# Block sums formed a slice per group, a second output tile begun early, and three smaller moves in a transformer trunk

## The chip, the cores and the metric

The kernel runs on one core of one Trainium2 chip. A core has TensorE (PE, with its weight loads as PEld), VectorE (DVE), ScalarE (ACT), GpSimd (POOL) and SyncE (SP, which here issues most of the transfers). The metric is the device time of one execution in microseconds; less is better.

## The reference

One pre-norm layer with D = 1024 and 2048 tokens, all in float32:

```python
xn = rms_norm(x, mix_norm_g[l]);  h = xn @ w_in[l]
q, k, v, f_logit, z = jnp.split(h, ...)             # 8 heads of 64; z has 2 x 512
log_f = jax.nn.log_sigmoid(f_logit + b_f[l])
attn = forgetting_attention(q, k, v, log_f)         # logit + cumsum(log f)[t] - cumsum(log f)[s], causal
sgu = spatial_gating(jax.nn.gelu(z), ...)           # zu * (chunk-causal mix of layer_norm(zv) + b)
merged = concat([rms_norm(attn, g_a), rms_norm(sgu, g_b)])
x = x + merged @ w_out[l]
gate, up = jnp.split(rms_norm(x, ffn_norm_g[l]) @ w_gate_up[l], 2)
x = x + (silu(gate) * up) @ w_down[l]               # d_ff = 2816
return rms_norm(x, final_norm_g)
```

## The kernel before

**Arithmetic.** Each float32 operand is split into a high and a low part (`hi_of`, a cast, mostly on ACT, L129; `lo_of`, the remainder, on DVE, L132), and each product is three matmuls: high by high, high by low, low by high. The program writes operations in an order of its own; a scheduler places them on each engine's queue, held by `behind(...)`, which names an instruction that has to come first, and by the buffers of the tile pools. An engine runs its queue in order.

**Projections (0 to about 350 us).** Four chunks of 512 tokens. In each, eight tiles of q and k (`L576`), the v tiles (`L458`) and the forget gates are formed. From chunk 1 on, the maxima of the attention logits of the chunk before are taken between the k steps of these tiles: `one_max` is one matmul (L361) and one reduction on DVE (L363 or L366); its operands A, B and D are read back from DRAM where q, k and the gate rows were stored shortly before. `n_early` is the number of maxima per tile, worked out from the table `EB`.

**Attention (to about 960 us).** `units` lists pairs of a head h and a query chunk j; each has 4j + 4 steps, one per block of 128 keys, 320 in all. A step is the logits (L735, L736, bank `mx_ps`), the exponential on ACT (`Pt`, L738), its split (`Ph` on ACT, `Pl` on DVE), on the diagonal blocks an affine select of each on POOL (L748), and two steps later the product with V (L768 to L773, tile `tp`). As filler between the steps TensorE gets the gating projection (`gates`, L927), whose side work `u_side` transposes the gated tiles `zr` into bank `z`, copies them on ACT into `wsth` or `wstl` (one buffer each, L998) and stores them to ST. From step `OPEN` the preparation of the first two output tiles (`out_prep`) runs, one `yield` per step: normalised rows are squared on ACT (L1092), POOL adds the squares (L1094, L1095), TensorE sums them over partitions (L1108) and broadcasts the root (L1113). Tile 0's product with the left half of `w_out` is begun between the last steps (`out_product`, `pz`). The other output tiles follow (`out_tiles`), and `out_done` turns each into normalised columns, stored to XT (to about 1098 us).

**FFN (from about 1098 us).** Up and Down run as products of 2 x 2 blocks with seven products and block sums in place of eight. There are five sets: 1 and 2 are Up for one half of the tokens each (22 items, in groups of two), 3, 4 and 5 are Down for a third of d_ff each (8 items). In a group each of the seven slots has two items of 12 matmuls (9 in set 5). The moving operands R0 to R6 (high and low) stay for a whole set and are refilled in its last group for the next: `staged` loads the four blocks of 1 MB into `sg0` to `sg3`, and `refill` splits blocks and forms their sums there on DVE and POOL (L1352, table `TE`). The weights of a group (`raw`, or HD in Down) are loaded some groups ahead, their sums formed (L1352) and split. `evac` takes a finished product from its bank `pp`; `done` (queued in `posts`) forms the last RMSNorm of a tile of rows: square on ACT (L1515), root on DVE and POOL, scaling on DVE (L1540), store.

## Time and profile before

| | |
|---|---|
| median of three executions | 2375.95 us (2375.18 to 2379.35) |
| the profiled execution | 2381.17 us |
| its span, first to last instruction | 2379.4 us |
| granted TensorE clock, mean | 0.996 |
| busy share: PE, DVE, ACT, POOL | 98%, 70%, 44%, 26% |
| HBM traffic | 253 MB read, 125 MB written |

In a row of the timeline stand the start, the duration (for xN from the first start to the last end), the engine, the line, the operation, what it writes <- what it reads, and in brackets the idle time of the engine before it and what ended that. "issue" as the one who ended a wait means that the profile shows none. SPq is SP's queue of transfers.

### The profile page before, as it was taken

The numbers are of one execution on the slowest core, as the hardware profiler recorded it, in microseconds if no ns is written. First come the engines' busy times: TensorE is split into PE (matmuls) and PEld (weight loads), VectorE is DVE, ScalarE is ACT, GpSimd is POOL, SyncE is SP. The second block draws the span as 40 slices with busy tenths as digits, with TensorE's granted clock in tenths as the row PEclk, the third lists the DMA queues.
The fourth block names the chain that finished last, engine by engine and source line by source line (L and its number), as shares of the span: only waits on it lengthen the run. The fifth ranks groups of instructions, "written<-read, shape, count | busy, mean of one in ns | idle before, by whom it ended". The sixth has DMA issues, their size and how long they took to land. (4 is left out here: it accounts for less than half of the span.)

```text
span 2379.4 us, 31425 instructions
## 1 busy us (share of the span) xinstructions
PE 2340.1 (98%) x10582; PEld 1894.4 (80%) x10582; DVE 1669.8 (70%) x2736; ACT 1055.7 (44%) x1770; POOL 623.3 (26%) x705
## 2 busy tenths in 40 slices
PE   9999999999999989999999999999999999999997
PEld 7778777777777768788888888788888878888886
DVE  6658668888888666467655656965555696696888
ACT  5322138777787766344323233432323242332433
POOL 1100012122121222221323323232322325354531
PEclk9999999999999999999999999999999999999999
DMA  8845667655687865666233232423232245455453
GB/s 271 284 154 193 205 206 207 180 161 156 191 211 237 223 206 168 216 214 199 71 89 92 80 94 76 151 83 89 72 89 82 80 141 186 167 186 200 152 190 148
DMA packets 358152, 380.60 MB, mean 160 GB/s; under 512 B 22292, under 2 KB 275924, under 8 KB 355432
## 3 DMA queue, kind: packets, MB, share of 16 engines
q1 hardware_dynamic: 342008, 335.36, 46.6%
q0 software_dynamic: 7616, 27.33, 3.3%
q10 hardware_dynamic: 8368, 15.91, 1.8%
q8 instruction: 85, 1.39, 0.3%
q14 instruction: 75, 0.61, 0.1%
HBM read 253.35 MB, written 125.18 MB: 159 GB/s over the span
## 5 line engine op out<-in xcount | busy, mean ns | idle before, releaser
L129 ACT CAST wh<-raw 128x512 fp32r<-128x512 f32 (+2 forms) x492 | 302.1, 621 | 748.3 <-PE pp L1663 608.3
L132 DVE TENSOR_TENSOR wl<-raw,wh 128x512 fp32r<-128x512 f32 (+2 forms) x496 | 373.2, 762 | 82.0 <-ACT wh L129 81.5
L1663 PE MATMUL pp<-wl,wh 128*128 128x512 f32 x1056 | 325.4, 389 | 1.2 <-ACT u L1418 1.0
L1663 PE MATMUL pp<-wh,wh 128*128 128x512 f32 x1056 | 325.4, 389 | 0.0
L1352 POOL TENSOR_TENSOR raw<-raw 128x512 f32<-128x512 f32 (+1 forms) x124 | 163.6, 1321 | 510.0 <-DMA raw<-in_w_gu_dram 357.9
L132 DVE TENSOR_TENSOR Pl<-Pt,Ph 128x512 fp32r<-128x512 f32 (+1 forms) x320 | 195.2, 615 | 80.4 <-ACT Ph L129 77.5
L1663 PEld LDWEIGHTS pp<-wl,wh 128*128 128x128 f32 x1056 | 198.1, 188 | 43.0 <-ACT u L1418 1.4
L1663 PEld LDWEIGHTS pp<-wh,wh 128*128 128x128 f32 x1056 | 198.2, 188 | 41.2
L738 ACT ACTIVATE Pt<-mx_ps 128x512 f32<-128x512 f32 (+1 forms) x320 | 169.2, 533 | 124.9 <-PE mx_ps L736 120.7
L1663 PE MATMUL pp<-wl,wl 128*128 128x512 f32 x528 | 205.8, 390 | 1.0 <-DVE wl L132 1.0
L1663 PE MATMUL pp<-wh,wl 128*128 128x512 f32 x528 | 205.4, 389 | 0.0
L927 PE MATMUL z<-wh,xz 128*128 128x512 f32 x496 | 188.9, 397 | 0.0
L1352 DVE TENSOR_TENSOR raw<-raw,raw 128x512 f32<-128x512 f32 (+1 forms) x112 | 132.1, 1181 | 77.7 <-POOL raw L1352 74.2
L129 ACT CAST Ph<-Pt 128x512 fp32r<-128x512 f32 (+1 forms) x320 | 175.9, 557 | 19.3 <-PE tp L770 3.8
L363 DVE TENSOR_REDUCE mx<-mx_ps 128x1 f32<-128x512 f32 x192 | 129.9, 682 | 20.5 <-PE mx_ps L361 20.0
L748 POOL TENSOR_SCALAR_AFFINE_SELECT Ph<-Ph 128x128 fp32r<-128x128 f32 x128 | 52.8, 413 | 314.4 <-DVE Pl L132 219.6
L768 PE MATMUL tp<-Ph,V 128*128 128x512 f32 (+1 forms) x320 | 118.8, 371 | 3.7 <-POOL Ph L748 2.6
L735 PE MATMUL mx_ps<-A,D 74*128 74x512 f32 (+1 forms) x320 | 119.3, 373 | 2.9 <-ACT Pt L738 2.9
L361 PE MATMUL mx_ps<-D,A 66*128 66x512 f32 (+2 forms) x320 | 118.6, 373 | 2.6 <-issue 2.0
L773 PE MATMUL tp<-Pl,V 128*128 128x512 f32 (+1 forms) x320 | 118.6, 370 | 1.3 <-POOL Pl L748 0.9
L736 PE MATMUL mx_ps<-B,C 128*128 128x512 f32 (+1 forms) x320 | 117.5, 368 | 0.0
L1663 PEld LDWEIGHTS pp<-wl,wl 128*128 128x128 f32 x528 | 99.1, 188 | 22.6 <-DVE wl L132 2.1
(340 smaller groups left out, 5301.7 us busy)
## 6 DMA issues: line engine op xcount, KB each, us to landing
raw<-in_w_gu_dram SPq DMA_DIRECT2D x88, 512.0 KB
xz<-XS SPq DMA_DIRECT2D x31, 1024.0 KB
HD<-hT SPq DMA_DIRECT2D x44, 512.0 KB
D<-KH SPq DMA_DIRECT2D x112, 128.0 KB
XA<-xa SPq DMA_DIRECT2D x27, 512.0 KB
raw<-HD SPq DMA_DIRECT2D x24, 512.0 KB
XA<-xb SPq DMA_DIRECT2D x21, 512.0 KB
xa<-XA SPq DMA_DIRECT2D x20, 512.0 KB
```

What stands on the lines that cost most here:

```text
L129: return nc.scalar.copy(o, i) if eng is nc.scalar else eng.tensor_copy(o, i)
L132: return eng.tensor_tensor(o, i, f(h), ALU.subtract)
L361: last_mx.append(nc.tensor.matmul(pm[:, 0:n], lhs, Dt[0 : lhs.shape[0], 0:n], start=True, stop=True))
L363: nc.vector.tensor_reduce(mx[:, a, s : s + 1], pm, AX.X, ALU.max)
L735: nc.tensor.matmul(st[:, off:], Dt[:, b * P : (b + 1) * P], A[:, off:], start=True, stop=False)
L736: nc.tensor.matmul(st[:, off:], C[:, b * P : (b + 1) * P], B[:, off:], start=False, stop=True)
L738: nc.scalar.activation(Pt[:, off:], st[:, off:], AF.Exp)
L768: nc.tensor.matmul(pv[:, off:], V[:, 0:P], Ph[:, off:], start=kb == 0, stop=False)
L773: nc.tensor.matmul(pv[:, off:], V[:, 0:P], Pl[:, off:], start=False, stop=kb == 4 * j + 3)
L927: nc.tensor.matmul(pz, xz[a][:, k, :], w[b][:, k, :], start=n == 0, stop=n == 3 * KT - 1)
L1352: (nc.vector if e == "v" else nc.gpsimd).tensor_tensor(o, a, b, op)
L1663: nc.tensor.matmul(pm, a[:, k, :], b[:, k, :], start=on is None and k == 0 and e == 0, stop=k == it.kh - 1 and e == 2, skip_group_check=n ...
```

## The change

**Maxima.** In chunk 1 the first q tile (pr = 0) takes no maxima; the others take four per tile instead of three.

**Order of units and opening.** The last eight units were heads 6, 7 as 7's j = 0, 1, then 6's four, then 7's j = 2, 3. Now they are (6,0), (7,0), (6,1), (7,1), (6,2), (6,3), (7,2), (7,3). The output preparation opens at step 260, not 265, and has more pauses where it has its own buffer.

**Second output tile.** The left half of tile 1 is also begun between the last steps: its eight products, an own load of its x (`x01[1]`), and its addition.

**Last gating tiles.** For the last q of `u_side` the four transposed tiles go through `mx_ps` banks and into four parts of one tile (tag `zvh`) instead of `wsth` and `wstl`.

**Block sums.** The sums of a set's blocks are no longer formed in its refill. In the groups of sets 1 and 2, `block_sums` takes one slice k of all four blocks in each of 15 rounds: four loads into two `xa` tiles, four operations on DVE, and in the next group two stores to the DRAM tile `SM`. The refill fetches seven ready blocks (three of w_down or XT, four of SM: the fourth of these for the position that formerly came last of the sums), four ahead and three in place of blocks already kept.

**Tail.** In the last group the posts run in another number per slot, held behind the last evacuation of each slot.

The matmuls are the same in number and kind.

```diff
-EB = [1, 12, 12, 12]
+EB = [1, 11, 12, 12]
-OPEN = 265
+OPEN = 260
...
-                    with behind(*maxima(n_early, k)):
+                    with behind(*maxima(n_early if c > 1 or which or pr else 0, k)):
...
+        last = q == NCH - 1
+        if last:
+            z4 = T(p2z, [P, 4, 4, P], F32, "zvh", bufs=1)
         for cc in range(4):
...
-            tp = T(psz, [P, 4, P], F32, "z", bufs=NZ)
+            tp = T(ps2, [P, 4, P], F32, "mx_ps", bufs=NMX) if last else T(psz, [P, 4, P], F32, "z", bufs=NZ)
...
-            sT = T(p2z, [P, 4, P], F32, ("wsth", "wstl")[cc % 2], bufs=1)
+            sT = z4[:, cc] if last else T(p2z, [P, 4, P], F32, ("wsth", "wstl")[cc % 2], bufs=1)
...
-    units = units[:-8] + units[-4:-2] + units[-8:-4] + units[-2:]
+    units = units[:-8] + [(h, j) for j in range(2) for h in (H - 2, H - 1)] + units[-6:-4] + units[-2:]
...
         for _ in range(2 if wg and left else 0):
-            out_product(pz, 0, 0, left.pop(0), s0)
-            if not left:
-                nc.vector.tensor_tensor(x0, x0, pz, ALU.add)
+            t, k = left.pop(0)
+            if k == K_OUT[0]:
+                pz = T(psz, [P, CH], F32, "z", bufs=NZ)
+                if t:
+                    x01.append(T(p2, [P, CH], F32, "jk", bufs=1))
+                    ld(x01[1], x[P : 2 * P, 0:CH])
+            out_product(pz, t, 0, k, None if t else s0)
+            if k == K_OUT[-1]:
+                nc.vector.tensor_tensor(x01[t], x01[t], pz, ALU.add)
...
+    def source(s, n):
+        if n in (0, 2, 6):
+            return block(s, {0: 0, 2: 2, 6: 3}[n])
+        return SM[s][:, {1: 0, 4: 1, 5: 2, 3: 3}[n], 0 : sets[s - 1][0].kh]
...
+    def block_sums():
+        last = None
+        for s in (2, 3, 4, 5):
+            for k in range(sets[s - 1][0].kh):
+                n, p = yield
+                while n != 2 or NF // 2 < p < NF // 2 + 2:
+                    n, p = yield
+                if last:
+                    with behind(hd[-1]):
+                        put(*last)
+                while n != 3 or NF // 2 - 1 <= p < NF // 2 + 2:
+                    n, p = yield
+                t = [T(xap, [P, D], F32, "xa") for _ in range(2)]
+                b = [t[i // 2][:, (i % 2) * CH : (i % 2 + 1) * CH] for i in range(4)]
+                with behind(*hd[-1:]):
+                    for i in range(4):
+                        ld(b[i], block(s, i)[:, k])
+                while n != 5:
+                    n, p = yield
+                tt("v", b[1], b[3], b[1], ALU.subtract)
+                tt("v", b[0], b[0], b[1], ALU.add)
+                n, p = yield
+                tt("v", b[2], b[2], b[0], ALU.subtract)
+                tt("v", b[3], b[3], b[0], ALU.subtract)
+                last = s, k, t
...
-    def refill(sg, kh, te):
-        ...
-        yield keep(0, b11)
-        tt(te[1], b11, b11, b12, ALU.add)
-        yield keep(1, b11)
-        yield keep(2, b21)
-        tt(te[2], b21, b21, b11, ALU.subtract)
-        tt(te[3], b11, b22, b11, ALU.subtract)
-        yield keep(3, b11)
-        ...
+    def refill(s, sg):
+        kh = sets[s - 1][0].kh
+        for n in range(7):
+            r = keep_as(n, sg[n], kh)
+            if n < 3:
+                sg.append(fetch(s, n + 4))
+            yield r
...
-        for _ in range(len(its)):
-            while posts and next(posts[0], 0) == 0:
-                posts.pop(0)
+        tail = p == len(grp) - 1
+        with behind(*[its[0].last] if tail and n else ()):
+            for _ in range((2, 2, 2, 2, 0, 1, 1)[n] if tail else len(its)):
+                while posts and next(posts[0], 0) == 0:
+                    posts.pop(0)
+            if tail and n == 6:
+                next(posts.pop(), None)
```

Three places show what moves. The first is DVE in the last group of set 2, where the operands of set 3 are formed: `sg` are the blocks, `R1l`, `R3l`, `R4l` (and the tiles named `wh`, `wl` of 128x2048) the low halves kept, `u` and `c` products in work. Before:

```order
L132 TENSOR_TENSOR wh_12188<-sg_3821_15724,wh_12188 128x2048
L1465 TENSOR_TENSOR u_18288<-u_18288,pp_18309 128x512
L1465 TENSOR_TENSOR u_18292<-u_18292,pp_18322 128x512
L1352 TENSOR_TENSOR sg_3821_15724<-sg_3821_15724,sg_3822_15725 128x2048
L132 TENSOR_TENSOR wl_18343<-raw_4243_18163,wh_18342 128x512
...
L132 TENSOR_TENSOR R1l_18339<-sg_3821_15724,R1h_18338 128x2048
...
L1352 TENSOR_TENSOR sg_3823_15726<-sg_3823_15726,sg_3821_15724 128x2048
L132 TENSOR_TENSOR wl_18421<-raw_4243_18163,wh_18420 128x512
L1352 TENSOR_TENSOR sg_3821_15724<-sg_3824_15727,sg_3821_15724 128x2048
```

Now:

```order
L131 TENSOR_TENSOR wh_12192<-sg_4142_17576,wh_12192 128x2048
L1519 TENSOR_TENSOR u_18473<-u_18473,pp_18496 128x512
L1519 TENSOR_TENSOR u_18477<-u_18477,pp_18509 128x512
L131 TENSOR_TENSOR wl_18531<-raw_4278_18348,wh_18530 128x512
L131 TENSOR_TENSOR wl_18535<-raw_4280_18352,wh_18534 128x512
L131 TENSOR_TENSOR R1l_18525<-sg_4143_17578,R1h_18524 128x2048
```

The three sums of 128x2048 are gone; the weights' splits (`wl` from `raw`) and those of R1 follow the evacuations at once.

The second is POOL at the opening of the output tiles: `zvl` are the squares of tiles 0 and 1, `rar` their roots, `Ph` and `Pl` the selects of the last diagonal steps. Before:

```order
L1094 TENSOR_TENSOR zvl_9643<-zvl_9643 128x256
L1095 TENSOR_TENSOR zvl_9643<-zvl_9643 128x128
L748 AFFINE_SELECT Ph_9778<-Ph_9778 128x128
L748 AFFINE_SELECT Pl_9780<-Pl_9780 128x128
L748 AFFINE_SELECT Ph_9792<-Ph_9792 128x128
L748 AFFINE_SELECT Pl_9794<-Pl_9794 128x128
L177 TENSOR_TENSOR rar_9807<-raa_9805,mhalf_206 128x1
L748 AFFINE_SELECT Ph_9820<-Ph_9820 128x128
L748 AFFINE_SELECT Pl_9822<-Pl_9822 128x128
L1094 TENSOR_TENSOR zvl_9643<-zvl_9643 128x256
L1095 TENSOR_TENSOR zvl_9643<-zvl_9643 128x128
```

Now:

```order
L1097 TENSOR_TENSOR zvl_9526<-zvl_9526 128x256
L1098 TENSOR_TENSOR zvl_9526<-zvl_9526 128x128
L1097 TENSOR_TENSOR zvl_9526<-zvl_9526 128x256
L1098 TENSOR_TENSOR zvl_9526<-zvl_9526 128x128
L748 AFFINE_SELECT Ph_9778<-Ph_9778 128x128
L748 AFFINE_SELECT Pl_9780<-Pl_9780 128x128
L176 TENSOR_TENSOR rar_9791<-raa_9789,mhalf_206 128x1
L176 TENSOR_TENSOR rar_9797<-raa_9795,mhalf_206 128x1
```

Both pairs of additions stand ahead of the last four diagonal steps; before, tile 1's pair stood behind three of them.

The third is DVE at the end of the program: `sg2` is the last tile of rows, `r4a` the start of a root, L1540 (now L1596) the scaling of a finished row tile. Before:

```order
L1540 SCALAR_TENSOR_TENSOR xa_4836_21443<-xa_4836_21443,r4r_4933_21851,sg0_4715_20896 128x1024
L1420 TENSOR_TENSOR u_4931_21847<-u_4931_21847,pp_4936_21859 128x512
L175 TENSOR_SCALAR r4a_4939_21884<-ss4_4937_21871 128x1
L1352 TENSOR_TENSOR sg2_4930_21844<-sg2_4930_21844,u_4931_21847 128x512
L1540 SCALAR_TENSOR_TENSOR sg1_4894_21697<-sg1_4894_21697,r4r_4940_21886,sg0_4715_20896 128x1024
L1423 TENSOR_TENSOR sg2_4930_21844<-sg2_4930_21844,pp_4929_21834 128x512
L1425 TENSOR_TENSOR sg2_4930_21844<-sg2_4930_21844,pp_4941_21890 128x512
L1510 TENSOR_SCALAR a5_4942_21901<-a5_4942_21901 128x1
L1511 TENSOR_TENSOR sg2_4930_21844<-sg2_4930_21844,sg0_4715_20896 128x512
L175 TENSOR_SCALAR r4a_4947_21921<-ss4_4944_21906 128x1
L1540 SCALAR_TENSOR_TENSOR sg1_4894_21697<-sg1_4894_21697,r4r_4948_21923,sg0_4715_20896 128x1024
L1427 TENSOR_TENSOR u_4931_21847<-u_4931_21847,pp_4946_21909 128x512
```

Now:

```order
L1596 SCALAR_TENSOR_TENSOR xa_4880_21635<-xa_4880_21635,r4r_4977_22043,sg0_4759_21088 128x1024
L1474 TENSOR_TENSOR u_4975_22039<-u_4975_22039,pp_4982_22054 128x512
L1415 TENSOR_TENSOR sg2_4974_22036<-sg2_4974_22036,u_4975_22039 128x512
L174 TENSOR_SCALAR r4a_4983_22066<-ss4_4978_22047 128x1
L1477 TENSOR_TENSOR sg2_4974_22036<-sg2_4974_22036,pp_4973_22026 128x512
L1596 SCALAR_TENSOR_TENSOR sg1_4938_21889<-sg1_4938_21889,r4r_4984_22068,sg0_4759_21088 128x1024
L174 TENSOR_SCALAR r4a_4987_22085<-ss4_4985_22072 128x1
L1564 TENSOR_SCALAR a5_4990_22102<-a5_4990_22102 128x1
L1565 TENSOR_TENSOR sg2_4974_22036<-sg2_4974_22036,sg0_4759_21088 128x512
L1596 SCALAR_TENSOR_TENSOR sg1_4938_21889<-sg1_4938_21889,r4r_4988_22087,sg0_4759_21088 128x1024
L1479 TENSOR_TENSOR sg2_4974_22036<-sg2_4974_22036,pp_4989_22091 128x512
L1481 TENSOR_TENSOR u_4975_22039<-u_4975_22039,pp_4992_22107 128x512
```

Between the start of a root and the scaling that needs it stands now an addition or the square's own work, and the last scaling comes one addition earlier (ahead of L1479, before behind L1425).

## The prediction

> **What bounds the kernel now.** I read the page's first part, the stages in the view of windows, TensorE's waits for the whole span, then the windows and timeline around its longest gaps. A windows row gives: stretch, its length, busy us and count of PE, PEld, DVE, ACT and POOL, granted clock, DMA share, GB/s.

> ```profile
> PE 2340.1 (98%) x10582; PEld 1894.4 (80%) x10582; DVE 1669.8 (70%) x2736; ACT 1055.7 (44%) x1770; POOL 623.3 (26%) x705
> 0.00:350.00 350.00, 345.05 (x1550) 274.11 (x1551) 238.13 (x589) 117.35 (x172) 37.95 (x78) 1.00 0.66 219
> 350.00:962.00 612.00, 600.50 (x2848) 470.69 (x2847) 478.32 (x924) 450.80 (x821) 133.84 (x298) 0.99 0.69 193
> 1098.00:2379.40 1281.40, 1261.26 (x5549) 1040.72 (x5547) 873.93 (x1116) 434.76 (x697) 426.05 (x294) 1.00 0.39 124
> ```

> TensorE is busy 2340.1 of 2379.4 us, and the change takes no matmul away. What can be won is its 39.3 us of idle time (5.0 in the projections, 11.5 in the attention, 20.1 from the FFN to the end) and stretches at a lower clock. The idle time sits in few places; a row of waits gives total, times, longest:

> ```profile
> PE pp L1663 <- DVE wl L132: 4.0, 4, 2.3
> PE mx_ps L735 <- ACT Pt L738: 2.9, 4, 2.1
> PE pp L1663 <- ACT wh L129: 2.7, 2, 1.4
> PE mx_ps L1108 <- POOL zvl L1095: 2.2, 2, 1.3
> PE mx_ps L361 <- issue: 2.0, 1, 2.0
> PE pp L1663 <- ACT u L1418: 1.0, 1, 1.0
> ```

> A gap of two microseconds costs more than itself. Over the last stage a matmul takes 1261.26 / 5549 = 0.227 us. After the 2.02 us gap before the first maximum, two starts lie 0.43 us apart:

> ```profile
> 86.95 0.30 PE L361 MATMUL mx_ps<-D,A 66*128 66x128 f32 x1 [2.02 <-issue]
> ...
> 88.58 0.63 PE L576 MATMUL mm<-xh,wh 128*128 128x512 f32 x1
> 89.01 0.63 PE L576 MATMUL mm<-xl,wh 128*128 128x512 f32 x1
> ```

> The granted clock (third figure from the end) shows the same at three other places, and none of it behind a gap of 1.3 us at 1524:

> ```profile
> 840.00:850.00 10.00, 8.54 (x36) 6.57 (x36) 6.46 (x12) 5.77 (x11) 2.63 (x6) 0.83 0.16 45
> 870.00:880.00 10.00, 7.98 (x28) 6.38 (x29) 2.12 (x5) 3.94 (x8) 1.28 (x4) 0.83 0.74 237
> 1520.00:1525.00 5.00, 3.68 (x16) 2.47 (x14) 5.00 (x5) 1.33 (x3) 3.03 (x1) 1.00 0.68 209
> 1955.00:1960.00 5.00, 4.96 (x15) 3.95 (x16) 5.00 (x6) 1.84 (x3) 1.11 (x1) 0.66 0.65 218
> ```

> 0.17 of 10 us, or 0.34 of 5 us, is 1.7 us lost each time; with four places 6.8 us.

> [...]

> **First maximum a tile later.** TensorE stands at 86.95 because the maximum's operands are still arriving. With none in the first tile of chunk 1, it comes 21 matmuls later, 21 x 0.227 = 4.8 us, past the 2.0. Removed: 2.0 + 1.7 = −3.7. The rest of the chunk takes four maxima per tile instead of three, whose loads have one unit's lead; bounds −3.7 to +1 (one more 2.0 wait without a dip, say half of it net). I take −3.7, as the lead left (2.8 us) is longer than the gap.

> **Second tile early, unit order, opening five steps sooner.** Two places. In the output preparation TensorE waits for POOL's sums:

> ```profile
> 835.30 0.94 POOL L1094 TENSOR_TENSOR zvl<-zvl 128x256 f32<-128x256 f32 x1 [14.57 <-ACT zvl L1092]
> 837.10 0.38 PE L1108 MATMUL mx_ps<-ones_c,zvl 128*128 128x1 f32 x2 [1.29 <-POOL zvl L1095]
> 840.98 0.38 PE L1108 MATMUL mx_ps<-ones_c,zvl 128*128 128x1 f32 x2 [0.89 <-POOL zvl L1095]
> 842.64 0.40 PE L1113 MATMUL mx_ps<-ident,rar 128*128 128x128 f32 x1 [0.57 <-POOL rar L177]
> ```

> 1.29 + 0.89 + 0.57 = 2.75, plus the 1.7 behind 840. The changed order puts both pairs of sums ahead of the last diagonal selects and gives one more pause before each reader; a pause is about one attention step (612 us for 320 of them, 1.9), more than the longest wait. I keep 0.5 of the waits: −3.9 (bounds −4.4 and 0). Second:

> ```profile
> 860.00:866.00 6.00, 4.88 (x22) 2.60 (x22) 5.45 (x12) 5.23 (x13) 1.02 (x1) 1.00 0.91 271
> 870.88 0.58 ACT L998 COPY wsth<-z 128x512 f32<-128x512 f32 x1 [3.05 <-DMA ST<-wsth]
> 872.02 0.44 PE L735 MATMUL mx_ps<-A,D 74*128 74x384 f32 x1 [2.10 <-ACT Pt L738]
> ```

> ScalarE's copy of a gating tile waits 3.05 us for the store that reads its buffer; the exponential queued behind it is late and TensorE waits 2.10. With a buffer for each of the last four copies this wait cannot arise. The attention steps there also get 24 products more as filler (24 x 0.227 = 5.4 us of matmuls that stood in one run later, so no time of their own). 2.1 + 1.7, and half of the 1.1 us that TensorE idles in 860 to 866, is −4.3 (bounds −4.9 and 0). The added load of 256 KB, one add of 0.7 us on DVE and a copy on ScalarE lie beside these products. Against it: the twelve diagonal steps, whose selects on POOL come between exponential and product, now stand in one row instead of two; TensorE waits for these selects 2.6 + 0.9 us in the whole run, of which I let a fifth come again: +0.7.

> **Block sums.** At the end of a set DVE forms the next set's operands from whole blocks (ns: least, median, most):

> ```profile
> L1352 DVE TENSOR_TENSOR sg<-sg,sg x19: 1218/2279/3418, 1019.5 to 2239.2; 128x2048 f32<-128x2048 f32 x14, 128x1536 f32<-128x1536 f32 x3, 128x1024 f32<-128x1024 f32 x2
> 1912.00:1960.00 48.00, 43.97 (x185) 35.29 (x184) 47.34 (x42) 22.19 (x26) 14.83 (x8) 0.96 0.47 154
> 1950.94 4.04 DVE L132 TENSOR_TENSOR wl<-raw,wh 128x512 fp32r<-128x512 f32 x3
> 1955.04 0.50 PE L1663 MATMUL pp<-R3h,wl 128*128 128x512 f32 x1 [2.31 <-DVE wl L132]
> ```

> DVE is the late engine at the end of set 2: busy 47.34 of 48 us, while TensorE idles 4.0 and waits for DVE's splits. Three sums go, at 2.28 at least 6.8 us of DVE, against the 2.31 that its longest wait is late. All waits of pp together are 4.0 + 2.7 + 1.0 = 7.7, plus the dip's 1.7: 9.4 if every one goes. I take −8.3, one wait of about 1 us staying (bounds −9.4 and 0).

> The work returns in 15 rounds: four loads of 256 KB, four sums of 128x512 and two stores of 512 KB each; in all 60 sums, 103 more DMA issues on SP. The nearest rows for a round are these of an Up group:

> ```profile
> 1214.19 4.74 SPq L1481 DMA_DIRECT2D HD<-hT  x2
> 1223.86 0.69 DVE L1465 TENSOR_TENSOR u<-u,pp 128x512 f32<-128x512 f32 x1 [1.43 <-PE pp L1663]
> 1226.36 0.62 ACT L129 CAST wh<-raw 128x512 fp32r<-128x512 f32 x1 [2.10 <-PE pp L1663]
> 1227.73 8.90 SPq L1448 DMA_DIRECT2D raw<-in_w_gu_dram  x4
> 1231.71 1.29 POOL L1352 TENSOR_TENSOR raw<-raw 128x512 f32<-128x512 f32 x1 [13.18 <-DMA raw<-in_w_gu_dram]
> ```

> A sum costs DVE 0.68 alone; beside POOL three of that size took 4.04, or 1.35 each: 41 to 81 us over some 800, where DVE is 874 busy of 1281 in the last stage. The round's loads go out on SP between HD's stores (done at 1219) and the weight loads (1227.7), so they would land near 1230; the first two sums stand behind u's addition of 1223.9. Thus DVE may stand some 6 us, with weight splits queued behind the sums. TensorE lives meanwhile on five finished weight tiles of 12 matmuls, 5 x 12 x 0.227 = 13.6 us, less half a tile in work about 12; and ScalarE, whose casts wait for a bank of TensorE (2.10), isn't the limit. So nothing reaches TensorE. The weight loads go out about 5 us later, which POOL, 13.18 us idle before its sums, takes up. The last group of a set fetches three more blocks of 1 MB, each once DVE has kept the block that lay there; it is wanted four slots (4 x 24 x 0.227 = 22 us) later. I allow +1.0 for a cover that fails once. Bounds: −0 and 15 x (2 + 1.7) = +55 if every round fails.

> [...]

> **Tail.** TensorE's last matmul is that of 2366.76, but DVE runs behind:

> ```profile
> 2361.74 1.28 DVE L1540 SCALAR_TENSOR_TENSOR sg<-sg,r4r,sg 128x1024 f32<-128x1024 f32 x1 [0.44 <-POOL r4r L177]
> 2364.46 0.15 DVE L1510 TENSOR_SCALAR a<-a 128x1 f32<-128x1 f32 x1 [0.24 <-ACT jk L1515]
> 2365.64 0.15 DVE L175 TENSOR_SCALAR r4a<-ss 128x1 f32<-128x1 f32 x1 [0.43 <-ACT jk L1515]
> 2366.52 1.28 DVE L1540 SCALAR_TENSOR_TENSOR sg<-sg,r4r,sg 128x1024 f32<-128x1024 f32 x1 [0.73 <-POOL r4r L177]
> 2366.76 0.39 PE L1663 MATMUL pp<-wl,wl 128*128 128x512 f32 x1
> 2370.53 1.06 ACT L1515 ACTIVATE jk<-sg 128x1024 bf16<-128x1024 f32 x1 [4.93 <-issue]
> ```

> The changed order lets the squares start sooner and puts an addition into each of these four waits, 0.44 + 0.24 + 0.43 + 0.73 = −1.8 (bounds −2.6, when DVE keeps up with the last product, and +0.5). What follows the last addition, from the square at 2370.53 to the span's end 8.9 us, is untouched.

> **Sum:** −3.7 −3.9 −4.3 +0.7 −8.3 +1.0 −1.8 = −20.3. The profiled execution took 2381.2 (span 2379.4 and 1.8 around it), so 2360.9; it lies 5.2 over the median 2375.95, from which it would be 2355.7. I say 2358, between the two; its own range is 2353 to 2363.

> **Rivals.** *The dips stay* (12%). [...] The waits go, 6.8 us stay: 2365.

> *Half the gain* (16%). The late engine is late for another reason: at the end of set 2 the splits of the whole blocks, not the sums, fill DVE (47.34 − 6.8 leaves 40 of 48), and the fetches of the last three blocks now wait for the first three to be kept, with weight loads behind them on SP. Then half of 8.3 stays, and half of 8.2 in the attention: 2358 + 8 = 2366. Against it, the 6.8 us freed are more than the 4.0 that TensorE idles.

> *No change* (10%). Rounds cost about 1 us each, 15 in all: 2373, within 0.2% (4.75 us, about what can be told from no change).

> *Slower* (6%). The loads land later than some 12 us after u's addition, past 1236: then DVE, blocked at the first sum, lets the weight tiles run out in each round, 2 us and a dip of 1.7: 2358 + 55 = 2413; if half the rounds do, 2386. For it: two stores of the round before must land first. Against it: SP is idle from 1219 to 1227.7.

> My forecast has 56%. Faster by over 0.2% are it and the first two, 84%; same 10%; slower 6%. The lower bounds together, −3.7 −4.4 −4.9 −9.4 −2.6 = −25.0, make 2351 from the median. The range 2350 to 2371 takes that and the two partial cases in, and leaves out some of the last two.

> **What would show it.** No wait of L361 for issue near 87 and granted clock 1.00 there; no wait of over 0.5 us for zvl or behind wsth's store; at the end of set 2 DVE with idle time and pp's waits under 1.5 us together; in the Up groups DVE waiting for loads of xa while TensorE's row shows no gap; the last addition on DVE about 2 us sooner relative to the last product. The prediction is wrong if pp waits for wl in the middle of sets 1 and 2, or if the dips come without gaps.

## The result and the profile after

The changed kernel takes 2363.91 us (median of six, 2360.72 to 2365.33) against 2376.97 for the one before (six, 2371.74 to 2379.35): ratio 0.9946, interval 0.9934 to 0.9957, 13.1 us less. Beside the last experiments, in another session, the same two gave 0.9966 (0.9955 to 0.9977), 9.3 us less. The profiled executions differ by more, 2381.17 to 2363.86 or 17.3 us, since that of before was slower than each of its six timed ones. The working below is on the traces.

The page's first line and, from the windows, the stages of the changed kernel, with the columns of the prediction's rows:

```profile
PE 2332.7 (99%) x10582; PEld 1893.4 (80%) x10582; DVE 1673.4 (71%) x2781; ACT 1058.8 (45%) x1771; POOL 609.8 (26%) x704
```

```profile
0.00:350.00 350.00, 344.58 (x1550) 274.19 (x1551) 237.62 (x588) 117.42 (x172) 37.89 (x78) 1.00 0.65 219
350.00:962.00 612.00, 599.75 (x2859) 471.96 (x2857) 480.53 (x926) 451.87 (x822) 132.97 (x298) 1.00 0.69 194
1098.00:2362.00 1264.00, 1252.81 (x5526) 1035.80 (x5524) 871.20 (x1158) 432.00 (x690) 413.24 (x293) 1.00 0.50 159
```

TensorE's idle time fell from 39.3 to 29.3 us, and its busy time by 7.4, of which the clock is a part. The projections idle 5.4 us (5.0 before) and the attention 12.2 (11.5 before): nothing was won there in idle time. The last stage idles 11.2 instead of 20.1. What TensorE waits for in the changed kernel:

```profile
PE tp L768 <- POOL Ph L748: 3.6, 8, 1.1
PE mx_ps L1111 <- POOL rd L1098: 2.6, 2, 1.4
PE tp L773 <- DVE Pl L131: 2.5, 2, 1.9
PE mx_ps L360 <- DVE mx L365: 2.5, 1, 2.5
PE pp L1718 <- ACT u L1472: 1.0, 1, 1.0
PE mx_ps L1111 <- POOL zvl L1098: 0.8, 1, 0.8
PE pp L1718 <- DVE wl L131: 0.3, 1, 0.3
```

The waits of `pp` are nearly gone (7.9 with the smallest, to 1.5), those for issue and of 2.1 us for Pt too; in their place stand new ones, for a maximum's reduction, for Pl and for the squares `rd`.

Cut at the same instructions in both traces (an exponential, the silu or the copy of the same product, the last matmul's start; the first silu with the table load ahead of it), the stretches in us are as follows. The cut in the attention is the 284th of the 320 exponentials, which the expectations below call the 292nd.

| stretch | before | after | difference |
|---|---|---|---|
| to the first exponential | 328.7 | 328.8 | +0.1 |
| from it to the 284th | 530.9 | 530.8 | −0.1 |
| from there to the FFN's first silu | 257.7 | 252.4 | −5.3 |
| set 1 up to its end | 379.0 | 378.9 | −0.1 |
| end of set 1 | 78.7 | 76.2 | −2.5 |
| set 2 up to its end | 304.6 | 304.6 | 0.0 |
| end of set 2 | 108.4 | 102.5 | −5.9 |
| rest of Down, the end of set 3 in it | 378.7 | 377.8 | −1.0 |
| from the last matmul's start on | 12.7 | 10.0 | −2.7 |

**Where a new wait took the place of the old one.** The first maximum comes without a wait now, but the same gap stands 11 us later. Timeline of the changed kernel:

```profile
94.20 0.31 ACT L320 ACTIVATE v<-F 128x128 f32<-128x128 f32 x1 [4.09 <-DMA F<-FD]
94.53 1.28 ACT L321 ACT_TABLE_LOAD   x1
96.16 0.23 DVE L322 TENSOR_SCALAR v<-v 128x128 f32<-128x128 f32 x1 [4.67 <-ACT v L321]
97.50 0.49 DVE L365 CUSTOM_DVE_ANT_0 jk<-mx_ps,dmask 128x384 f32<-128x384 f32 x1
98.05 0.47 PE L360 MATMUL mx_ps<-D,A 66*128 66x128 f32 x1 [2.49 <-DVE mx L365]
```

Read upwards: TensorE wants a bank that the third maximum's reduction (97.50) has to free; the reduction stands on DVE behind the forget-gate rows (L322), these wait for ScalarE, and ScalarE waits for the gates to come back from DRAM and then loads a table. Before, four reductions stood ahead of these rows (then L323), and DVE stood only 0.87 us for them:

```profile
97.07 0.23 DVE L323 TENSOR_SCALAR v<-v 128x128 f32<-128x128 f32 x1 [0.87 <-ACT v L322]
```

In the changed kernel the windows show the gap and the half clock behind it, where the old place at 87 now runs full:

```profile
85.00:90.00 5.00, 5.00 (x24) 4.16 (x23) 2.75 (x6) 2.12 (x4) 1.12 (x2) 1.00 0.77 289
90.00:100.00 10.00, 7.51 (x30) 5.91 (x30) 4.79 (x14) 3.60 (x6) 1.82 (x4) 0.90 0.57 202
100.00:110.00 10.00, 10.00 (x45) 8.08 (x45) 8.98 (x30) 5.07 (x8) 2.24 (x5) 0.93 0.80 274
890.00:900.00 10.00, 10.00 (x40) 7.79 (x40) 8.53 (x13) 6.70 (x13) 0.34 (x1) 0.84 0.37 105
```

Two of the four stretches of lower clock are gone (840 and 1955 of before); the other two came back at 98 and at 890. The last follows the preparation of tiles 2 and 3, as the timeline shows; in the preparation of tile 0 DVE stands for a load of the normaliser with a Pl queued behind it:

```profile
831.90 0.69 DVE L1092 TENSOR_TENSOR raw<-raw,zvl 128x512 f32<-128x512 f32 x1 [3.78 <-DMA zvl<-RD]
833.25 0.50 PE L773 MATMUL tp<-Pl,V 128*128 128x512 f32 x1 [1.88 <-DVE Pl L131]
...
880.82 0.69 DVE L1092 TENSOR_TENSOR raw<-raw,rd 128x512 f32<-128x512 f32 x1 [1.08 <-DMA rd<-RD]
883.57 0.38 PE L1111 MATMUL mx_ps<-ones_c,rd 128*128 128x1 f32 x2 [1.14 <-POOL rd L1098]
888.09 0.38 PE L1111 MATMUL mx_ps<-ones_c,rd 128*128 128x1 f32 x2 [1.44 <-POOL rd L1098]
```

**Where the rounds went.** DVE stands for a round's loads, and TensorE does not notice. Timeline, group of the sums (ns least, median, most) and windows of set 1 up to its end:

```profile
1224.86 0.69 DVE L1415 TENSOR_TENSOR xa<-xa,xa 128x512 f32<-128x512 f32 x1 [4.95 <-DMA xa<-XT]
```

```profile
L1415 DVE TENSOR_TENSOR xa<-xa,xa x45: 681/691/694, 1145.5 to 1797.7; 128x512 f32<-128x512 f32 x45
```

```profile
1112.05:1490.92 378.87, 378.87 (x1674) 313.70 (x1673) 244.33 (x337) 123.28 (x204) 112.71 (x81) 1.00 0.48 142
```

A sum costs 0.69 us (the group has 45 of the 60; the other 15 read one tile alone), and TensorE is busy for the whole 378.87 us with nine rounds in them. Over the 15 rounds DVE stands 3.3 to 6.1 us for the loads.

### The profile page after: what moved, and what is told of

Same layout as the page of the kernel before. It is cut to its first block, busy times and chain, and to the rows that moved or that the text cites. A ratio compares the mean times of both kernels' runs of the same rounds, so it can differ in the third digit from the quotient of the medians.

```text
span 2362.0 us, 31692 instructions
## 1 busy us (share of the span) xinstructions
PE 2332.7 (99%) x10582; PEld 1893.4 (80%) x10582; DVE 1673.4 (71%) x2781; ACT 1058.8 (45%) x1771; POOL 609.8 (26%) x704
## 4 chain that ended last, share of the span: by engine, by line
PE 86%; DVE 5%; DMA 4%; ACT 3%; issue 2%; POOL 1%; SPq 0%; ACTq 0%; POOLq 0%; DVEq 0%
PE pp L1718 51%; PE z L927 5%; PE mm L575 5%; PE pp L1176 4%; PE mm L457 3%; PE mx_ps L360 2%; PE tp L768 2%; PE tp L773 2%; PE mx_ps L735 2%; PE mx_ps L736 2%; PE oz L1176 2%; PE tp L770 1%; DVE wl L131 1%; DVE Pl L131 1%; PE z L968 0%
## 5 line engine op out<-in xcount | busy, mean ns | idle before, releaser
L1415 POOL TENSOR_TENSOR raw<-raw 128x512 f32<-128x512 f32 (+1 forms) x124 | 173.0, 1397 | 565.4 <-DMA raw<-in_w_gu_dram 337.9
L738 ACT ACTIVATE Pt<-mx_ps 128x512 f32<-128x512 f32 (+1 forms) x320 | 169.1, 532 | 122.0 <-PE mx_ps L736 117.7
L735 PE MATMUL mx_ps<-A,D 74*128 74x512 f32 (+1 forms) x320 | 118.3, 370 | 0.5 <-ACT Pt L738 0.5
```

What stands on the lines that cost most here:

```text
L735: nc.tensor.matmul(st[:, off:], Dt[:, b * P : (b + 1) * P], A[:, off:], start=True, stop=False)
L738: nc.scalar.activation(Pt[:, off:], st[:, off:], AF.Exp)
L1415: return (nc.vector if e == "v" else nc.gpsimd).tensor_tensor(o, a, b, op)
```

## Experiments

The variants are edits of the changed kernel. "Last matmul" below is the start of the program's last one; 2352.0 in the changed kernel.

**1. Gate rows later.** Is the first gap moved, or a thing of the maxima themselves?

```diff
-        for _ in range(1 if j else 2):
+        for _ in range((2, 2, 1, 1)[j]):
             yield
         sm = T(p1, [P, 8, P], F32, "v")
```

> The change with one thing more: the forget-gate rows of chunk 1 are formed one q tile later. Theory (the gap did not go, it moved: the reduction of the third maximum stands on DVE behind the gate rows, which wait 4.67 us for ScalarE and through it for the gates' round trip through DRAM): the 2.49 us gap at 98 and the lower clock behind it both go, the first exponential comes near 324.6 instead of 328.8, the rest of the run is the same, 2359.7 in the terms of the changed kernel's profile (2363.9). Rival (chunk 1's maxima lack operands wherever they start, so a gap of about 2 us comes back at another place): the first exponential stays within 1 us of 328.8, the time near 2364.

Measured: 2361.17 us, ratio to the kernel before 0.9941 (0.9923 to 0.996). The first exponential is at 326.5, not 324.6: this execution was already 0.7 later at the gap's place, and from matmul 336 to 384 of the projections, around the gap, it needs 13.5 us where the change needs 16.9, so 3.4 less, as expected; 0.4 of it is lost again after. This trace also has two stretches of half clock in the attention (near 486 and 837) that the traced execution of the change has not, so its span is only 0.3 us shorter. A wait of 0.83 remains, without lower clock (its timeline, then its windows):

```profile
103.35 0.33 PE L360 MATMUL mx_ps<-D,A 66*128 66x128 f32 x1 [0.83 <-DVE mx L365]
```

```profile
90.00:100.00 10.00, 10.00 (x48) 8.28 (x47) 6.09 (x22) 4.06 (x7) 2.89 (x6) 1.00 0.80 294
100.00:110.00 10.00, 9.16 (x42) 6.84 (x41) 9.23 (x29) 5.73 (x8) 1.18 (x3) 1.00 0.79 276
```

The gate rows are the cause: the later maxima ran into DVE's stand.

**2. Block sums undone.** The refill of the kernel before is put back, with its table and its loads:

```diff
-        for n in range(7):
-            r = keep_as(n, sg[n], kh)
-            ...
+        yield keep(0, b11)
+        tt(te[1], b11, b11, b12, ALU.add)
+        ...
-    sums = block_sums()
+    sums = None
```

> The change with its block sums undone: whole-block sums at the end of each set, no rounds. Theory (the sums on DVE made TensorE wait at the set boundaries, and the rounds cost nothing): the stretches over the ends of sets 1, 2 and 3 are longer by 2.6, 5.9 and 1.3 us, waits of pp return to about 7.7 us with one stretch at lower clock, the Up groups between them take the same time to 0.1 us; 2373.7 against 2363.9. Rival (the gain in these stretches came from the other order of fetches and weight loads, and the rounds cost some of it): under 5 us longer, and the Up groups shorter.

Measured: 2374.68 us, ratio to before 0.9993 (0.9984 to 1.0003). The end of set 1 takes 78.6 us, that of set 2 107.9, the stretch of set 3 229.8 against 228.5: 2.4, 5.4 and 1.3 more than with the rounds. The Up groups take 379.0 and 304.6. Its waits:

```profile
PE pp L1730 <- DVE wl L132: 3.9, 4, 2.3
PE pp L1730 <- ACT wh L129: 2.0, 2, 1.2
PE pp L1730 <- ACT u L1482: 1.0, 1, 1.0
```

The theory holds: the whole sums were the cost, the rounds are free. This one part is worth 9.1 us by the traces; by the ratios it is 0.9993 − 0.9946 = 0.0047, or 11 us, and 6 us with the change's other ratio, 0.9966. So it carries most of what the change gains. For all the other parts together the medians leave 0.0007 of gain, which is not clear of nothing, while the traces of this kernel give them about 8 us in the attention and the tail. A trace is one execution, here the fastest of this kernel against the slowest of the one before; what evens this out in the others isn't shown.

**3, 4. What a round may cost.** Eight or four more operations on DVE behind the sums of each round, each the maximum of a tile with itself, which leaves the numbers as they are:

```diff
                 tt("v", b[3], b[3], b[0], ALU.subtract)
+                for _ in range(8):     # 4 in the second kernel
+                    tt("v", t[1], t[1], t[1], ALU.max)
                 last = s, k, t
```

> The change with eight more DVE operations of 128x1024 (about 1.2 us each, 9.6 us in all, idempotent) behind the four sums of each of the 15 rounds. Theory (only the lead of TensorE's weight tiles matters, some 12 us, and DVE has about 13 us free in a group of 38): TensorE waits little, under 1 us a round, the time within 10 us of 2364. Rival (DVE's standing for the loads and the sums already uses the lead up): TensorE waits about 5 us in each round and runs at lower clock behind it, 2364 + 15 x 6.7 = 2464.

> The change with four more DVE operations of 128x1024 (4.8 us in all) behind the four sums of each round. Theory (a round's room is DVE's own time in a group: 38.1 us less 24.6 of work less the 5.0 that it stands for the loads, about 8.5 us; eight operations of 9.6 us were over it): 4.8 fits, the nine groups of set 1 take 379 us as in the change, the time is 2364. Rival (what counts is the stretch in which DVE does nothing for TensorE in one piece, and any lengthening of it reaches TensorE): half of the loss with eight, about 28 us over set 1 and 2410 in all.

Measured with eight: 2457.26 us. Set 1 up to its end takes 435.0 us, 6.2 more for each of the nine rounds, and set 2 35.2 more, 5.9 for each of six. The theory fell, the rival's number came out. The waits and a timeline of this kernel:

```profile
PE pp L1720 <- ACT u L1519: 61.6, 14, 5.8
```

```profile
1286.06 0.69 DVE L1417 TENSOR_TENSOR xa<-xa,xa 128x512 f32<-128x512 f32 x1 [8.31 <-DMA xa<-XT]
```

DVE is near its limit there: in the 435.0 us it works 341.4, and it stands 58.5 for the loads of the nine rounds (42.7 in the change), up to 8.3 in one, as these are late too now. TensorE waits for u, which DVE frees late. With four more: 2373.11 us, set 1 at 389.6, 1.2 more for each round, set 2 at 308.2 (0.6). That is between the two forecasts. From 4.8 to 9.6 us of added work the price in set 1 grows by 5.0 a round, about one for one with the clock included. An estimate from these two points is that a round has room for 4.8 − 1.2 = 3.6 us of DVE work, and not for 8.5 or 12. With four, too, DVE stands longer for the loads (57.0 us in the nine rounds), so its own work alone is not the whole limit.

**5. Old buffers for the last gating tiles.**

```diff
-        last = q == NCH - 1
+        last = False
```

> The change with its own buffers for the last gating tiles undone: they go through bank z and wsth, wstl again. Theory (the exponential stood behind a copy that waited for the store reading its buffer): a wait of L735 for Pt of 1 to 2 us comes back between 850 and 880, with or without a stretch of lower clock, and the stretch from the 292nd exponential to the FFN (252.4 us in the change) is 2 to 4 us longer. Rival (the other unit order and the earlier opening have already moved the copies away from the late stores): no such wait, the stretch within 1 us.

Measured once: 2368.05 us. From the 284th exponential to the FFN 256.8 us, 4.3 more than the change; 1.7 of it is clock, as half rate lasts 6.8 us behind 888 where it lasts 3.4 in the change. But the wait of 2 us for Pt is not there; what comes back are small waits, and the one in the preparation of tile 2 is longer (timeline):

```profile
859.87 0.50 PE L735 MATMUL mx_ps<-A,D 74*128 74x512 f32 x1 [0.52 <-ACT Pt L738]
862.41 0.50 PE L773 MATMUL tp<-Pl,V 128*128 128x512 f32 x1 [0.31 <-DVE Pl L131]
888.96 0.58 PE L1111 MATMUL mx_ps<-ones_c,rd 128*128 128x1 f32 x2 [3.16 <-DMA C<-KL]
```

The buffers are worth some us there, but the 2.10 us wait of before is gone without them too: the unit order, the opening or the second tile took it away. Which of them is open. The unit order wasn't undone alone: with the opening at 260 the normaliser of chunk 0 would be read before it is written.

**6. One early tile.**

```diff
-            left, s0 = [(t, k) for t in range(2) for k in K_OUT], o[0]["s"]
+            left, s0 = [(t, k) for t in range(1) for k in K_OUT], o[0]["s"]
 ...
-                    if t < 2 and fh == 0:
+                    if t < 1 and fh == 0:
 ...
-                        if k % 2 == 1 or its[0] == 0:
+                        if k % 2 == 1:
```

> The change with its second early tile undone: only tile 0's left half is begun among the attention steps. Theory (tile 1's 24 products stood between the preparation of tiles 2 and 3 and the matmuls that read it; without them these matmuls come too soon): the two waits for rd near 885 (1.1 and 1.4 us) and the lower clock behind them go, the waits of the last attention steps stay away, and two waits of 1.4 and 0.8 us at the first finished tiles come back; the stretch from the 292nd exponential to the FFN is 250 to 252 us against 252.4, the time 2362 to 2364. Rival (the early products are what shortened that stretch from 257.7): 256 to 258, the time 2368 to 2369.

Measured: 2360.04 us, ratio to before 0.9937 (0.9922 to 0.9953). The stretch to the FFN takes 251.5 us, in the theory's range and not 256 to 258: the rival falls. The two waits for rd and the lower clock behind them are gone; waits of 0.5, 0.3 and 0.6 us are back before them, with one of 0.57 at the first finished tile in place of the 1.4 and 0.8 expected. But ten traces of kernels with both tiles have 251.3 to 254.1 us in this stretch, and the other one with a single tile (experiment 11) has 252.7. So no gain or loss of the second early tile stands clear of single executions here. The window there reads:

```profile
870.00:900.00 30.00, 29.97 (x144) 23.88 (x143) 18.90 (x32) 20.52 (x39) 7.33 (x15) 1.00 0.88 244
```

**7. More pauses in the preparation.** Experiment 1 and:

```diff
-        for _ in range(4):
+        for _ in range(4 if space is None else 6):
             yield
         nc.vector.tensor_tensor(r[:, 0:4, :], r[:, 0:4, :], rd, ALU.mult)
 ...
-        for _ in range(3 if space is None else 5):
+        for _ in range((5 if t < 4 else 3) if space is None else 5):
```

> The change with the gate rows of chunk 1 a tile later, two more pauses between the loads and the first use in the preparation of tiles 0 and 1, and two more between POOL's sums and the matmul that reads them in that of tiles 2 and 3. Theory (each of these waits is a reader that comes too soon, and the delay falls where nothing is queued behind it): the waits of 2.5 us at 98, of 1.9 and 0.6 at 833 to 837, of 1.1 and 1.4 near 885 go, and two stretches of lower clock; 3.4 + 2.5 + 4.3 = 10 us less than the change, 2354 from 2363.9. Rival (the preparation is on time only as a whole: what is put off at its start waits at its end, at the first products of tiles 0 and 2): only the 3.4 us of the gate rows, 2360.5.

Measured: 2361.18 us, ratio 0.9939 (0.9926 to 0.9951), the gain of experiment 1 alone. The waits stand where they were, and two became one:

```profile
831.96 0.50 PE L773 MATMUL tp<-Pl,V 128*128 128x512 f32 x1 [1.84 <-DVE Pl L131]
886.98 0.38 PE L1111 MATMUL mx_ps<-ones_c,rd 128*128 128x1 f32 x2 [2.91 <-POOL rd L1098]
```

DVE's row has L1092 in the same place as without the pauses: the scheduler puts it there all the same (why isn't shown), and a pause in the program's text doesn't move it. Neither theory put it so; the rival's time came out.

**8. Posts of the last group as before.**

```diff
-            if at == len(grp) - 1:
-                yield
 ...
-        tail = p == len(grp) - 1
+        tail = False
```

> The change with the posts of the last group as before. Theory (the squares and scalings stood in DVE's row so that it was late after the last product): from the last matmul's start to the span's end 12.6 us as before, against 10.0. Rival (that end is shorter because of the other buffers and fetches): 10.0 to 10.9.

Measured once: from the last matmul's start to the end 11.9 us, against 10.0 with the change and 12.7 before. DVE has the waits of 0.43 and 0.73 again, and its last addition comes later (below them):

```profile
2352.25 0.15 DVE L174 TENSOR_SCALAR r4a<-ss 128x1 f32<-128x1 f32 x1 [0.43 <-ACT jk L1569]
2353.13 1.28 DVE L1594 SCALAR_TENSOR_TENSOR sg<-sg,r4r,sg 128x1024 f32<-128x1024 f32 x1 [0.73 <-POOL r4r L176]
2356.98 0.68 DVE L1487 TENSOR_TENSOR sg<-sg,pp 128x512 f32<-128x512 f32 x1
```

The last matmul starts at 2354.6 here, so this addition starts 2.4 us after it. With the new order it starts 0.53 to 0.57 us after it in all twelve traces, and before it started 3.6 after. The order of the posts is worth the 1.9 us from 2.4 to 0.5; what gives the other 1.2 wasn't taken apart. The end itself is a weaker measure: it comes 9.3 to 11.0 us after the last matmul's start in the twelve.

**9, 10. Gaps made on purpose.** Does a gap cause the lower clock? In 16 groups of sets 1 and 2 ScalarE repeats the copy of a finished bank, and the next matmul waits for the last of these:

```diff
+        if n == 0 and p in GAPS:
+            for _ in range(GAPS[p]):
+                held = nc.scalar.copy(its[-1].u, its[-1].ps[0])
 ...
+                    if held:
+                        pace(mm, held)
```

> The change with gaps put into TensorE's row: in 16 Up groups ScalarE repeats a copy of a finished bank 1 to 8 times, and the next matmul waits for the last one, which gives gaps of about 1 to 5 us in otherwise full groups. Theory (a gap of 2 us or more makes TensorE run at half rate for about 3.4 us, 1.7 us lost, a shorter one does not): each group is longer by its gap where the gap is under about 1.8 us, and by its gap plus 1.7 us from 2 us on, with granted clock under 1 only there. Rival 1 (the lower clock of the four places had a cause of its own): groups are longer by the gap alone whatever its length, clock 1.00. [...]

> As in the first run with gaps, with 16 gaps of 1.6 to 3.4 us only. Theory (a free-running window of about 3.4 us: a gap lowers the clock when enough of one window falls into it): none of the four gaps of 1.6 us is followed by half rate, about half of those of 2.2 us, two thirds or more of those of 2.8 and 3.4 us. Rival (a fixed length decides): each length gives the same answer every time.

Measured once each, 2446.81 and 2432.45 us. The gaps are 1.58 us and steps of 0.62 more. Windows of 10 us that begin where a gap ends, first kernel (behind gaps of 2.82 and 4.06), then second (2.20, 1.58 and 2.82):

```profile
1260.90:1270.90 10.00, 10.00 (x44) 8.29 (x45) 2.45 (x4) 2.37 (x4) 1.29 (x1) 1.00 0.79 267
1346.78:1356.78 10.00, 10.00 (x37) 8.12 (x38) 3.72 (x6) 1.36 (x3) 0.00 (x0) 0.83 0.50 166
```

```profile
1179.48:1189.48 10.00, 10.00 (x37) 8.13 (x38) 1.66 (x3) 1.37 (x3) 0.00 (x0) 0.83 0.70 232
1221.05:1231.05 10.00, 10.00 (x44) 8.29 (x45) 1.87 (x4) 2.37 (x4) 0.00 (x0) 1.00 0.78 248
1304.45:1314.45 10.00, 10.00 (x32) 8.04 (x33) 2.08 (x4) 1.24 (x2) 0.00 (x0) 0.70 0.85 275
```

A granted clock of 0.83 over 10 us is 1.7 us lost, 0.70 is 3.0; seven of 44 matmuls are missing in the one, twelve in the other. Over both kernels:

| gap, us | followed by lower clock |
|---|---|
| 1.58 | 0 of 5 |
| 2.20 | 6 of 8 |
| 2.82 | 6 of 7 |
| 3.44 | 4 of 5 |
| 4.06 and more | 7 of 7 |

Gaps cause it, so the rival in which it has a cause of its own falls. But no length between 2.2 and 3.4 decides: the same gap is followed by lower clock in one group and not in the next, 2.20 us in six of eight and 3.44 in four of five (the theory of the second run had about half and two thirds or more); the last section shows where such gaps lie on the grid of 3.413 us at which the clock changes. The theory of the first run (always from 2 us on) was too strict, and the fixed length of the second falls.

**11, 12. The two repairs together, and the change once more beside it.** Experiments 1 and 6 in one kernel; and the change as it is.

> The change with the gate rows of chunk 1 a tile later and its second early tile undone. Theory (two separate waits that the change itself put in: 2.5 us and a stretch of lower clock at 98, two waits and a stretch of lower clock near 885): 3.4 us and some 3 us less than the change on the same chip, ratio to the kernel before near 0.992, no wait over 1 us between 90 and 110 nor between 870 and 900. Rival (undoing the second tile only seemed to help, since single executions of one kernel differ by 4 us): only the 3.4 us of the gate rows, ratio 0.9935.

> The change as it is, once more, beside the others on the same chip: ratio 0.9946 as measured first, and in its profile the same stages (FFN groups to 0.1 us), so that differences of a few us between the variants can be told from those between executions.

Measured beside each other: 2357.81 us (2355.25 to 2361.47), ratio to before 0.993 (0.9918 to 0.9943), against 2366.02 us (2362.03 to 2370.07), 0.9966 (0.9955 to 0.9977) of the change, which is not the 0.9946 expected. The two intervals are apart: the repaired version beats both kernels, by 17.5 and 8.2 us of median. The 8.2 is nearer to the theory's 6.4 than to the rival's 3.4, though the ratio alone would fit the rival's 0.9935 too. Its windows at the two places:

```profile
90.00:110.00 20.00, 19.17 (x87) 15.05 (x87) 15.34 (x49) 9.86 (x14) 4.06 (x9) 1.00 0.79 277
870.00:900.00 30.00, 29.97 (x143) 23.76 (x143) 19.62 (x34) 19.78 (x37) 7.28 (x15) 1.00 0.90 245
```

In the one profiled execution of each the difference is only 3.5 us (spans 2356.7 and 2360.2), and that of the change was the fastest of its seven. Their mean clocks are 0.995 to 0.997 in the change and 0.998 or 0.999 in the repaired version. 0.002 of 2360 us is 4.7 us, so the rest of the 8.2 is likely clock in part: gaps that lower it in some executions only. Waits differ too: the two traces of the change differ by 2.0 us between the first and the 284th exponential, with full clock there in both, and one has a wait of 1.12 us at 710 that the other has not. Only one execution of each kernel in a session is traced, so the rest of the 8.2 stays open.

## Why the prediction was right or wrong

The time lies 5.9 us above the forecast of 2358, inside the range of 2350 to 2371, and faster as forecast; of 20.3 us of sum the traces show 17.4, the medians 13.1 and 9.3. That the sum came so near is partly luck: in the traces two terms fell short, by 3.8 and 2.2 us, and two went beyond, by 2.2 and 0.9.

- **First maximum, −3.7: wrong, 0 measured** (+0.1 to the first exponential). The step that failed is "I take −3.7, as the lead left (2.8 us) is longer than the gap". It looked at the operands of the first maximum, and not at what else stands on DVE, which has to reduce each maximum before TensorE has a bank for the next but one. Five us later is the time of the gate rows and their stand of 4.67 us. Experiment 1 gives the 3.4 us back when they are moved out of the way. The bound of +1 with "one more 2.0 wait" was the case that came.
- **Attention, −3.9 −4.3 +0.7 = −7.5: −0.1 up to the 284th exponential, −5.3 behind it.** The two pairs of sums are in place and their waits for zvl fell from 2.2 to 0.8, the wait for wsth's store is gone; that much was right. But the place of the −3.9 (835 to 843) lies in the first of these stretches, and almost nothing of it arrived there in the compared traces: DVE stands 3.78 us for the normaliser's load of tile 0, which costs 1.9 and 0.6 us at Pl. Tiles 2 and 3 are prepared sooner and cost 1.1 + 1.4 us and a lower clock. Neither was priced: the step named the waits that go and let only the diagonal steps come back. These steps' waits were 3.5 us before and are 3.4 to 4.6 in the traces of the changed order, so the +0.7 can't be told from nothing. The waits of 1.4 and 0.8 us at the first finished tiles, which the sum left in, went too, and are part of the −5.3. That the own buffers alone made the 2.10 wait go was argued too narrowly (experiment 5).
- **Block sums, −8.3: right, −9.5 measured** in the five FFN stretches together, 9.1 of it by experiment 2. The +1.0 for a cover that fails once was not needed. The sums cost 0.69 us each, 41 us in all, with POOL idle beside all 60 of them; so the 81, for sums beside POOL, was not put to the test here. (Of the three operations behind the 4.04 us two took 1.77 and 1.74 us and one 0.68, so 1.35 each is only their mean.) "DVE may stand some 6 us" was 3.3 to 6.1, and "nothing reaches TensorE" holds to 0.1 us over nine rounds. The lead of 12 us in that step was too large, though: experiments 3 and 4 put the room at some 3.6 us more in a round, an estimate, since DVE's own time in a group, less what it stands for the loads, is used up before the finished weight tiles are. The slower rival was nearer than it looked.
- **Tail, −1.8: the right mechanism for part of it, −2.7 measured.** Three of the four waits are gone, of the fourth, 0.73, there is 0.44 left: 1.4 us. The last addition on DVE starts 0.5 us after the start of the last matmul, where it was 3.6 after it, so 3.1 us sooner; the other 1.7 DVE has won already when it comes to these waits, which the step had only as its bound of −2.6, "when DVE keeps up with the last product". First the last addition before, then three rows of the changed kernel:

```profile
2370.37 0.68 DVE L1433 TENSOR_TENSOR sg<-sg,pp 128x512 f32<-128x512 f32 x1
```

```profile
2348.09 1.28 DVE L1596 SCALAR_TENSOR_TENSOR sg<-sg,r4r,sg 128x1024 f32<-128x1024 f32 x1 [0.44 <-POOL r4r L176]
2352.00 0.39 PE L1718 MATMUL pp<-wl,wl 128*128 128x512 f32 x1
2352.54 0.68 DVE L1487 TENSOR_TENSOR sg<-sg,pp 128x512 f32<-128x512 f32 x1
```

- **The clock, 1.7 us for each of four gaps.** The size was right: half rate lasts 3.41 us in each of the six places of the two compared traces, which is 1.7 us lost. Two of the four came back behind new gaps, so the rival's time of 2365 was nearly met, but not as "The waits go, 6.8 us stay" has it: with the dips came new waits. For a gap of some 2 us the 1.7 is an expectation, with 2.20 us six cases in eight (experiments 9 and 10), and no certainty.
- **Profiled or median.** The prediction took the middle between 2360.9 and 2355.7. The profiled pair differs by 17.3 us and the medians by 13.1, because the profiled execution of before was slower than every timed one of that session. The 5.9 us are 2.9 missing in the traces, 4.2 from profile to median and 1.0 by which the median of before rose with more executions, less the 2.3 by which the forecast already lay above 2355.7.

## What to carry to other kernels

When an instruction is moved to dodge a wait, list what stands at its new time on the engine that consumes its result, not only whether its operands have come: here DVE's stand of 4.67 us turned a 2.0 us gap into one of 2.5. Work that makes the late engine wait at a boundary can be spread in slices over groups where that engine is idle, and was free here as long as that engine had time left in a group: with nine rounds of four sums of 0.69 us in it set 1 took 378.9 us against 379.0, and with 4.8 us more in each round 389.6. Where a scheduler places the instructions, a pause in the program's text may move nothing, as L1092 in experiment 7; the order on the engine has to be looked at.

## What the hardware did that was not expected

| gap, us | kernel, start | idle in the grid's pieces, us | half rate |
|---|---|---|---|
| 3.44 | first, 1683.93 | 1.85 + 1.59 | none |
| 2.82 | first, 1260.90 | 1.00 + 1.82 | none |
| 2.82 | second, 1711.70 | 0.95 + 1.86 | 3.41 us |
| 2.20 | first, 1218.14 | 2.18 + 0.02 | 3.41 us |
| 2.82 | second, 1304.45 | 2.01 + 0.81 | 6.83 us |

In all 32 the same holds: the 23 gaps that left 1.86 us or more of idle time in one piece were followed by half rate from the end of that piece, and the nine that left 1.85 or less in each were not. In all the traces, the program's start and end left out, half rate lasted two pieces instead of one where at least 0.67 us of idle time fell into its first piece, and one where it was 0.57 or less; that is the 3.0 us instead of 1.7. The row of the last gap's half rate:

```profile
1303.64:1310.47 6.83, 6.02 (x14) 4.82 (x15) 0.49 (x1) 1.34 (x3) 0.00 (x0) 0.50 0.83 271
```

In the attention, where small matmuls and small gaps are mixed, no one figure separates the cases: 1.05 us in a piece was followed by half rate at 489 in one trace, 1.56 at 830 was not in another. Near 486, where all the kernels run the same code, three traces have half rate (1.05 to 1.09 us idle in the piece before) and the others have none, among them four with 0.98 to 1.04. So the same instructions can meet half rate in one execution and not in the next. That this makes up the spread of one kernel (the change by 8.0 us in seven executions) isn't shown.
